# A 64-row matmul between the two passes of one block, in the second unit of both MLPs

## The chip, the cores and the metric

The kernel runs on one core of one Trainium2 chip. The metric is the device time of one execution in microseconds, as the median of several runs. Three runs of the kernel before took 2397.16, 2397.32 and 2398.94 us; the median is 2397.32 us. TensorE (PE) does the matmuls into PSUM, VectorE (DVE) and ScalarE (ACT) do the elementwise work, SyncE (SP) issues nearly all the loads.

## The reference, cut to what matters

Two layers of a decoder trunk over 256 positions of width 2048, in fp32. Each layer is a mixing part (attention and RWKV-7 in layer 0, RG-LRU and HGRN2 in layer 1) and then an MLP with squared ReLU:

```python
def _sq_relu_mlp(h, w1, w2):          # w1: 2048 x 8192, w2: 8192 x 2048
    z = jax.nn.relu(h @ w1)
    return (z * z) @ w2

x = x + _sq_relu_mlp(_rms_norm(x, norm_mlp[layer]), w_ff1[layer], w_ff2[layer])
```

The change touches only the two MLPs, and what it adds feeds none of these values.

## The kernel before, in words

Activations lie transposed: 16 tiles of 128 features by 256 positions. To keep nearly fp32 precision with single-pass matmuls, every operand is split into a rounded high part and the remainder. A moving tile is 512 columns wide: 256 of the high part, 256 of the low one.

A **unit** makes one 128-feature output tile from 16 **blocks** (`unit`, lines 155 to 161). A block handles one 128x128 piece of the weight and has two passes (`mm3`, lines 146 to 153): the **512 pass** (line 152) multiplies the high part `wh` with all 512 columns, the **256 pass** (line 153) multiplies the remainder `wl` with the 256 high columns. Both add into one PSUM bank. Each pass first loads its own 128x128 weights into the array (the PEld rows of the profile), so a block is: load `wh`, 512 pass, load `wl`, 256 pass.

The weights come in halves of a unit, 128x1024 fp32 or 512 KB. SP loads a half (line 125), ACT casts it to `wh` (line 130), DVE subtracts to get `wl` (line 132); two buffers of each exist. After the last block ACT and DVE add the two halves of the bank (lines 167, 168) and DVE applies the norm's factor and the squared ReLU.

One MLP (`mlp`) is 128 units, 64 up (`w_ff1`) and 64 down (`w_ff2`), in quarters `q` of 16 units: up(0), up(1), down(0), up(2), down(1), up(3), down(2), down(3). That is 2048 blocks per MLP. The norm before an MLP ends in one fp32 matmul with a matrix of ones (`rstd_of`, line 206, tile `ms_m`); PE runs an fp32 matmul as two rows of the trace. The scheduler places it inside the first unit, since the unit itself does not need the norm's factor.

Elsewhere fp32 matmuls of other shapes are put between the blocks of units too. In layer 0, line 425 (tile `pair`) multiplies 64-row operands with 128 columns; for each of eight head pairs it issues four such matmuls on the lower and four on the upper 64 rows. Line 350 (`lora`) uses 96 rows. The instruction order on each engine is fixed when the program is built.

Of the kernel before, what the change touches and what calls it, by code (L numbers as in the profile page):

```python
# [19 lines left out]
P = 128  # L20
T = 256
D = 2048
KT = D // P
# [35 lines left out]
def kernel(  # L59
# [20 lines left out]
    V, A, M, G = nc.vector, nc.scalar, nc.tensor, nc.gpsimd  # L80
# [19 lines left out]
    def c_(name):  # L100
        a, b = CON[name]
        return con[:, a:b]

    ident, bones, ones = c_("ident"), c_("bones"), c_("ones")
# [7 lines left out]
    def bank(name, tag="ga"):  # L112
        return pg.tile([P, 512], F32, tag=tag, name=name)
# [4 lines left out]
    def operand(pool, name):  # L118

        return [t[:, k] for t in (half_of(pool, f"{name}_{h}") for h in range(2)) for k in range(8)]  # L120
# [14 lines left out]
    def stream(src, name, pool=None):  # L135

        out = []
        for h in range(2):
            with tc.high_priority():
                out.append(split(load(src, h, name, pool if h else None), h, name))  # L140
        return out
# [5 lines left out]
    def mm3(ps, wh, wl, mv, first, last, folded=False):  # L147
        if folded:
            M.matmul(ps[:, :T], wh, mv[:, :T], start=first, stop=False)  # L149
            M.matmul(ps[:, :T], wh, mv[:, T:], start=False, stop=False)  # L150
        else:
            M.matmul(ps, wh, mv, start=first, stop=False)  # L152
        M.matmul(ps[:, :T], wl, mv[:, :T], start=False, stop=last)  # L153

    def unit(src, mv, name, folded=False, tag=None, parts=None, pool=None):
        ps = bank(f"mm_{name}", tag) if tag else pmm.tile([P, 512], F32, tag="mm", name=f"mm_{name}")
        parts = parts or stream(src, name, pool)
        for k in range(KT):
            wh, wl = parts[k // 8]
            mm3(ps, wh[:, k % 8], wl[:, k % 8], mv[k], k == 0, k == KT - 1, folded)  # L160
        return ps

    def evac(ps, name):
        t = ev.tile([P, T], F32, tag="t", name=f"t_{name}")
        s = ev.tile([P, T], F32, tag="s", name=f"s_{name}")
        with tc.high_priority():
            A.copy(t, ps[:, T:])  # L167
            V.tensor_add(s, ps[:, :T], t)  # L168
        return s
# [11 lines left out]
    def split_to(dst, src):  # L181
        A.copy(dst[:, :T], src)
        V.tensor_sub(dst[:, T:], src, dst[:, :T])
# [38 lines left out]
    def norm(name):  # L222
        acc = ev.tile([P, T], F32, tag="acc", name=f"acc_{name}", bufs=1)
        hx = operand(big, f"hx_{name}")
        return acc, hx
# [6 lines left out]
    def layer0_mix():  # L232
        with ExitStack() as st:
# [14 lines left out]
            with tc.tile_pool(name="pa", bufs=1) as pa:  # L248
# [3 lines left out]
                with tc.high_priority(10**6):  # L252
# [19 lines left out]
                    for i in range(2):  # L272
                        for j in range(8):
                            prepare(hx, 8 * i + j, xi[i][:, j], "gmix0")
                            if j == 3:
                                parts.append(split(raws[i], i, "i0_0"))
                    first.append(unit(None, hx, "i0_0", parts=parts))
                    squares(0)
                    parts = [split(raws[2], 0, "i0_1")]
                    squares(1)  # L280
                    parts.append(split(raws[3], 1, "i0_1"))
                    first.append(unit(None, hx, "i0_1", parts=parts))
                    squares(2)
                    squares(3)
                    rstd = rstd_of(acc, "a0")
                first.append(unit(w_in0[2], hx, "i0_2", tag="ga"))
                first.append(unit(w_in0[3], hx, "i0_3", tag="gb"))
                rwkv_a(pa, gate, hx, scaled_by(rstd), rwp_d, pm_d, nb, first, load_cw)
# [645 lines left out]
    def mlp(layer, xs, hx, rstd, nxt, zp, zraw):  # L934
        z = {}

        def up(q):
            zq = z[q] = operand(big if q % 2 == 0 else zp, f"z_{layer}_{q}")
            for k in range(KT):
                n = f"f1_{layer}_{q}_{k}"  # L940
                s = evac(unit(w_ff1[layer, q * KT + k], hx, n, pool=zraw), n)
                V.tensor_mul(s, s, rstd)  # L942
                V.scalar_tensor_tensor(s, s, 0.0, s, ALU.max, ALU.mult)
                split_to(zq[k], s)

        def down(q):
            for c in range(KT):
                n = f"f2_{layer}_{q}_{c}"
                s = evac(unit(w_ff2[layer, q, c], z[q], n, pool=zraw), n)
                V.tensor_add(xs[:, c], xs[:, c], s)  # L950
                if q == 3:
                    nxt(c)

        up(0)
        up(1)
        down(0)
        up(2)
        down(1)
        up(3)
        down(2)  # L960
        down(3)
# [7 lines left out]
    acc, hx = norm("m0")  # L969
# [11 lines left out]
    acc, hx = nacc  # L981
# [3 lines left out]
    acc, hx = norm("m1")  # L985
# [148 lines left out]
```

## Time and profile before

| what | us |
|---|---|
| median of three runs | 2397.32 |
| profiled execution, its own time | 2415.31 |
| its span, first to last instruction | 2413.5 |
| PE busy, share of the span | 99% |
| mean granted TensorE clock | 0.997 |

The profiled execution is one execution with the profiler on; it is 18.0 us longer than the median, and its time is 1.8 us longer than its span. In the rows, a start is counted in us from the first instruction. A matmul's own duration reaches past the start of the next one, because matmuls are pipelined; the distance between starts is what the engine needs. A line such as `x8` merges eight instructions that stand in a row.

### The profile page before, as it was taken

Reading aid. Unit: us, or ns where it says so; the run is one execution under the profiler, and the core shown is the slowest. Engines: PE = TensorE matmul, PEld = TensorE weight load, DVE = VectorE, ACT = ScalarE, POOL = GpSimd, SP = SyncE. Lnnn points to the kernel's source line nnn. Section 1 sums busy time; section 2 is a strip of 40 time slices with the busy share of each in tenths; the row PEclk is TensorE's granted clock in tenths of the full one; section 3 lists DMA queues with packets and bytes.
Section 4 is the critical chain, followed back from the end, with each engine's and each line's share of the span. In section 5 each row is a group of like instructions: output and inputs, shape, how many; then the busy total and the mean of one; then the engine's idle time right before and its main releaser. Section 6 shows DMA issues by size and latency. Waiting matters only on the chain.

```text
span 2413.5 us, 37947 instructions
## 1 busy us (share of the span) xinstructions
PE 2390.6 (99%) x14386; PEld 2072.1 (86%) x14386; DVE 1697.7 (70%) x3006; ACT 1243.7 (52%) x2152; POOL 44.9 (2%) x118
## 2 busy tenths in 40 slices
PE   8999999999999999999999999999999999999999
PEld 6888877798888888888888888889888888888888
DVE  7887865677676576576568888788777667667555
ACT  7554455555444444444456666675544444444443
POOL 0112010000000000000000000000000000000000
PEclk9999999999999999999999999999999999999999
DMA  7667743465555555655555444456556555656564
GB/s 263 212 216 228 246 139 105 155 209 183 190 184 186 188 184 187 188 185 187 187 176 187 150 151 153 154 168 217 185 191 191 189 188 191 192 187 190 191 199 134
DMA packets 125862, 446.77 MB, mean 185 GB/s; under 512 B 14192, under 2 KB 19952, under 8 KB 124016
## 3 DMA queue, kind: packets, MB, share of 16 engines
q1 hardware_dynamic: 115824, 414.06, 53.7%
q0 software_dynamic: 5456, 26.79, 3.1%
q10 hardware_dynamic: 4400, 3.50, 0.4%
q8 instruction: 114, 1.87, 0.3%
q14 instruction: 68, 0.56, 0.1%
HBM read 429.06 MB, written 15.22 MB: 184 GB/s over the span
## 4 chain that ended last, share of the span: by engine, by line
PE 93%; DVE 3%; DMA 2%; ACT 1%; issue 1%; POOL 0%; DVEq 0%; ACTq 0%; POOLq 0%
PE mm_f L152 39%; PE mm_f L153 20%; PE mm_i L152 13%; PE mm_i L153 7%; PE mm_o L153 2%; PE mm_o L152 1%; PE mm_o L149 1%; PE mm_o L150 1%; DVE wl_i L132 1%; PE hl L816 1%; PE pair L425 1%; DMA rwp<-rwp_d 1%; PE psx L496 0%; ACT wh_o L130 0%; PE psu L503 0%
## 5 line engine op out<-in xcount | busy, mean ns | idle before, releaser
L132 DVE TENSOR_TENSOR wl_f<-raw_f,wh_f 128x1024 fp32r<-128x1024 f32 x512 | 627.2, 1225 | 486.1 <-ACT wh_f L130 486.1
L130 ACT CAST wh_f<-raw_f 128x1024 fp32r<-128x1024 f32 x512 | 538.6, 1052 | 773.4 <-PE mm_f L152 566.8
L152 PE MATMUL mm_f<-hx_m,wh_f 128*128 128x512 f32 x2048 | 717.2, 395 | 0.0
L152 PE MATMUL mm_f<-z,wh_f 128*128 128x512 f32 x2048 | 717.1, 395 | 0.0
L152 PE MATMUL mm_i<-hx_a,wh_i 128*128 128x512 f32 x1536 | 563.9, 405 | 11.5 <-ACT wh_i L130 11.4
L153 PE MATMUL mm_f<-hx_m,wl_f 128*128 128x256 f32 x2048 | 574.8, 281 | 0.0
L153 PE MATMUL mm_f<-z,wl_f 128*128 128x256 f32 x2048 | 574.4, 280 | 0.0
L152 PEld LDWEIGHTS mm_f<-z,wh_f 128*128 128x128 f32 x2048 | 383.9, 187 | 90.0
L152 PEld LDWEIGHTS mm_f<-hx_m,wh_f 128*128 128x128 f32 x2048 | 383.9, 187 | 90.0
L153 PE MATMUL mm_i<-hx_a,wl_i 128*128 128x256 f32 x1536 | 447.6, 291 | 1.2 <-DVE wl_i L132 1.0
L153 PEld LDWEIGHTS mm_f<-hx_m,wl_f 128*128 128x128 f32 x2048 | 387.0, 189 | 0.1
L153 PEld LDWEIGHTS mm_f<-z,wl_f 128*128 128x128 f32 x2048 | 387.0, 189 | 0.0
L152 PEld LDWEIGHTS mm_i<-hx_a,wh_i 128*128 128x128 f32 x1536 | 289.8, 189 | 72.3 <-ACT wh_i L130 12.1
L153 PEld LDWEIGHTS mm_i<-hx_a,wl_i 128*128 128x128 f32 x1536 | 291.5, 190 | 9.3 <-DVE wl_i L132 4.0
L130 ACT CAST wh_i<-raw_i 128x1024 fp32r<-128x1024 f32 x192 | 201.3, 1049 | 188.9 <-PE mm_i L152 169.5
L132 DVE TENSOR_TENSOR wl_i<-raw_i,wh_i 128x1024 fp32r<-128x1024 f32 x192 | 234.5, 1222 | 80.6 <-ACT wh_i L130 76.4
L168 DVE TENSOR_TENSOR s_f<-mm_f,t_f 128x256 f32<-128x256 f32 x256 | 106.7, 417 | 3.0 <-ACT t_f L167 3.0
L132 DVE TENSOR_TENSOR wl_o<-raw_o,wh_o 128x1024 fp32r<-128x1024 f32 x64 | 78.3, 1223 | 32.6 <-ACT wh_o L130 32.3
L130 ACT CAST wh_o<-raw_o 128x1024 fp32r<-128x1024 f32 x64 | 67.2, 1050 | 63.3 <-issue 29.2
L167 ACT COPY t_f<-mm_f 128x256 f32<-128x256 f32 x256 | 93.2, 364 | 4.3 <-PE mm_f L153 4.3
L153 PE MATMUL mm_o<-ym,wl_o 128*128 128x256 f32 x256 | 72.6, 284 | 0.8 <-DVE wl_o L132 0.8
L942 DVE TENSOR_TENSOR s_f<-s_f,rstd_m 128x256 f32<-128x256 f32 x128 | 54.4, 425 | 4.4
(420 smaller groups left out, 2254.7 us busy)
## 6 DMA issues: line engine op xcount, KB each, us to landing
raw_f<-in_w_ff_dram SPq DMA_DIRECT2D x512, 512.0 KB, 4.5
raw_i<-in_w_in_dram SPq DMA_DIRECT2D x192, 512.0 KB, 4.1
raw_o<-in_w_out_dram SPq DMA_DIRECT2D x64, 512.0 KB, 4.2
rwp_d<-rwp POOLq DMA_DIRECT2D x8, 1026.0 KB, 7.1
rwp<-rwp_d POOLq DMA_DIRECT2D x4, 1540.0 KB, 10.7
cw<-in_cmp_w_dram SPq DMA_DIRECT2D x2, 2048.0 KB, 10.2
pm_d<-pm POOLq DMA_DIRECT2D x8, 512.0 KB, 6.3
pm<-pm_d POOLq DMA_DIRECT2D x4, 1024.0 KB, 5.3
```

What stands on the lines that cost most here:

```text
L130: A.copy(wh, raw)
L132: V.tensor_sub(wl, raw, wh)
L149: M.matmul(ps[:, :T], wh, mv[:, :T], start=first, stop=False)
L150: M.matmul(ps[:, :T], wh, mv[:, T:], start=False, stop=False)
L152: M.matmul(ps, wh, mv, start=first, stop=False)
L153: M.matmul(ps[:, :T], wl, mv[:, :T], start=False, stop=last)
L167: A.copy(t, ps[:, T:])
L168: V.tensor_add(s, ps[:, :T], t)
L425: M.matmul(pps[q][:, c * P : (c + 1) * P], bk[hs, c], ar[hs, c], start=True, stop=True)
L816: M.matmul(pl[:, x * T + i * P : x * T + (i + 1) * P], qk[:, ii], qk[:, ii], start=True, stop=True)
L942: V.tensor_mul(s, s, rstd)
```

## The change: what it does

In `mlp`, the unit with `q == 0` and `k == 1`, the second unit of each MLP, gets `part_at=4`. Its fifth block then issues its 512 pass, a new matmul of the identity's upper 64 rows with themselves (64 rows, 128 columns, fp32) into a PSUM bank of its own, and then its 256 pass. Nothing reads that bank.

```diff
+    def narrow(name):
+
+        ps = bank(f"nar_{name}")
+        tc.keep_in_program_order(M.matmul(ps[:, 0:P], ident[0:64], ident[0:64], start=True, stop=True))
+
-    def unit(src, mv, name, folded=False, tag=None, parts=None, pool=None):
+    def unit(src, mv, name, folded=False, tag=None, parts=None, pool=None, part_at=None):
...
         for k in range(KT):
             wh, wl = parts[k // 8]
+            if k == part_at:
+                M.matmul(ps, wh[:, k % 8], mv[k], start=False, stop=False)
+                narrow(name)
+                tc.keep_in_program_order(M.matmul(ps[:, :T], wl[:, k % 8], mv[k][:, :T], start=False, stop=False))
+                continue
             mm3(ps, wh[:, k % 8], wl[:, k % 8], mv[k], k == 0, k == KT - 1, folded)
...
-                s = evac(unit(w_ff1[layer, q * KT + k], hx, n, pool=zraw), n)
+                s = evac(unit(w_ff1[layer, q * KT + k], hx, n, pool=zraw, part_at=4 if q == 0 and k == 1 else None), n)
```

PE in the second unit of layer 0's MLP before, from the 256 pass of its fourth block on (`mm_f` is the unit's bank, `hx_m` the normed input, `wh_f` and `wl_f` the weights):

```order
L153 MATMUL mm_f_0_0_1_6222<-hx_m_0_5108,wl_f_0_0_1_0_6227 128x256
L152 MATMUL mm_f_0_0_1_6222<-hx_m_0_5108,wh_f_0_0_1_0_6225 128x512
L153 MATMUL mm_f_0_0_1_6222<-hx_m_0_5108,wl_f_0_0_1_0_6227 128x256
L152 MATMUL mm_f_0_0_1_6222<-hx_m_0_5108,wh_f_0_0_1_0_6225 128x512
L153 MATMUL mm_f_0_0_1_6222<-hx_m_0_5108,wl_f_0_0_1_0_6227 128x256
```

The same place on PE after the change (`nar_f` is the new bank, `con` holds the identity):

```order
L153 MATMUL mm_f_0_0_1_6222<-hx_m_0_5108,wl_f_0_0_1_0_6227 128x256
L166 MATMUL mm_f_0_0_1_6222<-hx_m_0_5108,wh_f_0_0_1_0_6225 128x512
L158 MATMUL nar_f_0_0_1_6244<-con 128x128
L168 MATMUL mm_f_0_0_1_6222<-hx_m_0_5108,wl_f_0_0_1_0_6227 128x256
L152 MATMUL mm_f_0_0_1_6222<-hx_m_0_5108,wh_f_0_0_1_0_6225 128x512
```

One row is new; the two passes around it only have new line numbers. In layer 1 the same single row is new at the same place of its second unit. No other row of any engine moves, and no instruction gets a new wait.

## Rows read from the trace of the kernel before

**Rows 1.** The page: busy time by engine; the chain that ended last, by engine.
```profile
PE 2390.6 (99%) x14386; PEld 2072.1 (86%) x14386; DVE 1697.7 (70%) x3006; ACT 1243.7 (52%) x2152; POOL 44.9 (2%) x118
...
PE 93%; DVE 3%; DMA 2%; ACT 1%; issue 1%; POOL 0%; DVEq 0%; ACTq 0%; POOLq 0%
```

**Rows 2.** Stretches, 512 passes alone: length, busy (count), PEclk, DMA share, GB/s.
```profile
600.00:1200.00 600.00, 600.00 (x1700) 319.12 (x1699) 1.00 0.59 186
1720.00:2320.00 600.00, 600.00 (x1732) 323.71 (x1731) 1.00 0.60 190
```

**Rows 3.** Groups, 566 to 1286 us (layer 0's MLP): busy, mean ns | idle before.
```profile
L152 PE MATMUL mm_f<-z,wh_f 128*128 128x512 f32 x1024 | 361.9, 399 | 0.0
...
L130 ACT CAST wh_f<-raw_f 128x1024 fp32r<-128x1024 f32 x253 | 265.7, 1050 | 385.3 <-PE mm_f L152 275.8 <-issue 109.5
```

**Rows 4.** Groups, 1703 to 2406 us (layer 1's MLP).
```profile
L152 PE MATMUL mm_f<-z,wh_f 128*128 128x512 f32 x1016 | 352.3, 391 | 0.0
...
L130 ACT CAST wh_f<-raw_f 128x1024 fp32r<-128x1024 f32 x253 | 266.6, 1054 | 381.5 <-PE mm_f L152 291.0 <-issue 90.5
```

**Rows 5.** Timeline of PE, first unit of layer 0's MLP: start, duration, instruction.
```profile
562.25 0.70 PE L206 MATMUL ms_m<-acc_m,con 128*128 128x256 f32 x2
562.60 0.47 PE L153 MATMUL mm_f<-hx_m,wl_f 128*128 128x256 f32 x1
```

**Rows 6.** Timeline of PE, first unit of layer 1's MLP.
```profile
1701.51 0.70 PE L206 MATMUL ms_m<-acc_m,con 128*128 128x256 f32 x2
1701.86 0.47 PE L153 MATMUL mm_f<-hx_m,wl_f 128*128 128x256 f32 x1
```

**Rows 7.** Timeline of PE, layer 0's input projection, 64-row matmuls before a 256 pass.
```profile
81.84 0.39 PE L152 MATMUL mm_i<-hx_a,wh_i 128*128 128x512 f32 x1
82.16 1.16 PE L425 MATMUL pair<-rwp,bk 64*128 64x128 f32 x8
83.25 0.39 PE L153 MATMUL mm_i<-hx_a,wl_i 128*128 128x256 f32 x1
83.47 0.39 PE L152 MATMUL mm_i<-hx_a,wh_i 128*128 128x512 f32 x1
```

**Rows 8.** Timeline of PE, the first two and last two of those eight.
```profile
82.16 0.49 PE L425 MATMUL pair<-rwp,bk 64*128 64x128 f32 x2
...
82.94 0.38 PE L425 MATMUL pair<-rwp,bk 64*128 64x128 f32 x2
```

**Rows 9.** Groups, 84.5 to 95.8 us, after the return of rows 7.
```profile
L152 PE MATMUL mm_i<-hx_a,wh_i 128*128 128x512 f32 x34 | 11.8, 391 | 0.0
```

**Rows 10.** Timeline of PE, a return from 64-row matmuls to a 512 pass.
```profile
175.07 0.72 PE L425 MATMUL pair<-rwp,bk 64*128 64x128 f32 x5
175.72 0.50 PE L152 MATMUL mm_i<-hx_a,wh_i 128*128 128x512 f32 x1
```

**Rows 11.** Groups, 177 to 186 us, after the return of rows 10.
```profile
L152 PE MATMUL mm_i<-hx_a,wh_i 128*128 128x512 f32 x25 | 8.9, 398 | 0.0
```

**Rows 12.** Timeline of PE, a return from 96-row matmuls to a 256 pass.
```profile
47.46 0.60 PE L350 MATMUL lora<-th,w 96*128 96x256 f32 x2
47.97 0.39 PE L153 MATMUL mm_i<-hx_a,wl_i 128*128 128x256 f32 x1
48.19 0.40 PE L152 MATMUL mm_i<-hx_a,wh_i 128*128 128x512 f32 x1
```

**Rows 13.** Groups, 39.6 to 46.6 and 49.5 to 56 us, before and after rows 12.
```profile
L152 PE MATMUL mm_i<-hx_a,wh_i 128*128 128x512 f32 x21 | 7.5, 399 | 0.0
...
L152 PE MATMUL mm_i<-hx_a,wh_i 128*128 128x512 f32 x20 | 7.0, 391 | 0.0
```

**Rows 14.** Timeline of PE, output projection of layer 1, after a short stall.
```profile
1613.24 0.39 PE L153 MATMUL mm_o<-ym,wl_o 128*128 128x256 f32 x1
1613.46 0.39 PE L152 MATMUL mm_o<-ym,wh_o 128*128 128x512 f32 x1
```

**Rows 15.** Groups, 1614 to 1620 us, after rows 14.
```profile
L152 PE MATMUL mm_o<-ym,wh_o 128*128 128x512 f32 x18 | 6.4, 399 | 0.0
```

**Rows 16.** Stretch from layer 0's MLP to layer 1's, 512 passes alone (columns of rows 2).
```profile
1290.00:1700.00 410.00, 323.48 (x883) 166.09 (x884) 1.00 0.52 170
```

## The prediction

> **What bounds the kernel now.** I read the page first: PE is busy for 99% of the span and makes 93% of the chain that ended last [rows 1], so what matters is how fast PE takes its blocks. Then I put one stretch of each MLP beside the other. They do the same work in the same code, yet 600 us hold 1700 512 passes in layer 0 and 1732 in layer 1 [rows 2]. A block thus takes 600/1700 = 352.9 ns in layer 0 and 600/1732 = 346.4 ns in layer 1: 6.5 ns apart (the two counts can be off by one, 0.2 ns each). The granted clock is 1.00 in both, the 2.4 GHz level [rows 2]. The groups by line give a fingerprint of the two cadences: a 512 pass lasts 399 ns on average in the slow one and 391 ns in the quick one [rows 3, 4]. Neither MLP lets PE wait: idle before the passes is 0.0 [rows 3, 4]. It is ACT that waits for PE to free weight buffers, 275.8 us in layer 0 and 291.0 us in layer 1 [rows 3, 4], so weights are not what makes layer 0 slow.
>
> What differs is the last disturbance before each stretch. In both MLPs it is the norm's matmul with full 128 rows, and PE returns from it through a 256 pass 0.35 us later [rows 5, 6]. The rows look alike, and yet one MLP stays slow for its whole length and the other quick. I read the cadence as something that a disturbance sets and that an undisturbed stream then keeps.
>
> **The change, part by part.** It removes nothing and moves nothing. It adds one 64-row fp32 matmul per MLP, which is a disturbance, and the question is which cadence follows.
>
> *The cadence after it.* The nearest rows are those of line 425, also 64 rows by 128 columns in fp32, between the passes of a unit. Where PE returns from them to a 256 pass [rows 7], the next stretch runs at 391 ns [rows 9]. There are three more such returns with a long stretch behind them (at 106, 129 and 152 us), and all run at 391. Where PE returns to a 512 pass [rows 10], the stretch runs at 398 ns [rows 11]; two more of these (at 200 and 227 us) run at 399. So with 64 rows the side of return decides: 4 of 4 quick through the 256 pass, 3 of 3 slow through the 512 pass. The change returns through the 256 pass. A quick cadence in layer 0 gives 6.5 ns for each block behind the insertion, of which there are 2048 - 16 - 5 = 2027: 2027 x 6.52 ns = 13.2 us. In layer 1 the stretch is quick already and stays so: 0.
>
> All four of these returns came from a quick stream, while layer 0's MLP is slow. The nearest row from a slow stream has 96 rows instead of 64: 399 ns before it, return through a 256 pass, 391 ns behind it [rows 12, 13]. The Trainium skill bears on this: "TensorEngine Tiling (Array Packing)", Key Properties, says that a change of tiling mode drains the engine. If so, the return would start from an empty array, and the cadence before would not matter; no row shows a 64-row matmul in a slow stream.
>
> *The cost of each insertion.* Rows 7 give the parts. From the 512 pass to the first 64-row row: 82.16 - 81.84 = 0.32 us. From the 256 pass to the next 512 pass: 83.47 - 83.25 = 0.22 us. The eight rows between take 83.25 - 82.16 = 1.09 us; they are four matmuls, two rows each, and the new one has two rows. The first two end at 82.65 and the last two at 83.32, and the 256 pass starts 0.07 us before that end [rows 8, 7]; so two rows alone take 0.49 - 0.07 = 0.42 us. Sum 0.32 + 0.42 + 0.22 = 0.96 us in place of 0.35 us: 0.61 us more. The bounds are 2/8 of 1.09 us, thus 0.27 in place of 0.42 (0.46 us more), and all 1.09 us (1.28 us more). I take 0.61 us, the value of rows of the same shape. Two insertions cost 1.2 us (0.9 to 2.6). All of it lies on PE, which has no idle time to hide it.
>
> *Weights at the quicker pace.* ACT and DVE must supply layer 0 at 346.4 ns a block; in layer 1 they do so with PE idle 0.0 and with ACT waiting 291.0 us for PE [rows 4]. I cost that at nothing. If the cover were gone, it would eat a part of the 13.2 us, never more.
>
> *What follows.* Layer 1's mixing part begins 13 us earlier and its stalls will fall otherwise. Its 883 512 passes [rows 16] run partly in each cadence; if half of them changed sides, that is 883/2 x 6.5 ns = 2.9 us either way. I take 0 and keep 2.9 us for the range.
>
> *The sum.* -13.2 + 1.2 = -12.0 us against the profiled execution: 2415.3 becomes 2403.3 us. The median of the runs is 18.0 us below the profiled time. If the runs have the same cadences as the profile, the profiler itself costs 18.0 us, and the median becomes 2397.3 - 12.0 = 2385.3 us.
>
> **The rivals.**
>
> *Both MLPs slow in the runs.* Nothing but a small difference around the norm's matmul seems to separate the MLPs [rows 5, 6], so layer 1 could be slow where no profiler runs. Then both insertions gain: -26.4 + 1.2, 2372.1 us. Against it: the profiler would then cost 18.0 + 13.2 = 31.2 us.
>
> *Nothing to repair.* Both MLPs are quick already in unprofiled runs; the 18.0 us by which the median lies below the profiled time has room for the 13.2 us. Then the insertions only cost: 2397.3 + 1.2 = 2398.5 us. The same time results if the cadence belongs to the place (buffers, addresses) and no disturbance changes it; against that stands that one projection with the same tiles shows both, 399 and 391 ns [rows 13]. The same time also results if a pass had a fixed distance to the next, as it has in neither MLP [rows 2]. The Trainium skill has such a rule: "TensorE: Matmul & The Clock Gate", Back-to-back issue gap, gives columns / 2.4 + 2.5 ns, an estimate of 325 ns for a block whatever came before; both measured cadences lie above it.
>
> *The restart falls slow.* The point that decides is the first two or three blocks behind the insertion. A return through a 256 pass after a short stall, with the same 0.22 us to the next 512 pass, was followed by 399 ns [rows 14, 15], and the return after the norm's matmul of layer 0 as well [rows 5, 3]. If both insertions end so, layer 0 stays slow and layer 1 loses its quick cadence: 13.2 + 1.2 = 14.4 us more, 2411.7 us. If only layer 1's does, layer 0's gain cancels it, and 2398.5 us results again. Against it: none of the four long 64-row returns to a 256 pass did this.
>
> **How the numbers follow.** I give the forecast (2385.3) a chance of 0.50, both MLPs slow (2372.1) 0.12, nothing to repair or one cancelling the other (2398.5) 0.24, the slow restart (2411.7) 0.14. Differences under 0.2%, 4.8 us, cannot be told from no change here. Faster: 0.50 + 0.12 = 0.62; same 0.24; slower 0.14. The likeliest case's own range is 2381 to 2390 us (the 2.9 us, the insertion's bounds, the counts). The range of 8 in 10 leaves out the slow restart and reaches over the other three with a small margin: 2370 to 2401 us.
>
> **What would show it.** In the profile of the changed kernel: the new matmul stands as two rows between a 512 and a 256 pass at about 567 us, with some 0.96 us from that 512 pass to the next. The 512 passes behind it average 391 ns, and 600 us of layer 0's MLP hold 1732 of them, not 1700. Layer 0's MLP ends about 12.6 us earlier, and layer 1's stays at 391 ns. The forecast is wrong if either MLP shows 399 ns behind its insertion, if PE starts to wait for weights, or if layer 0's MLP is quick and the time of the runs does not fall, which would mean that the runs were quick before.

## The result, and the profile after

The changed kernel takes 2426.17 us (median of four runs, 2425.75 to 2426.64); the kernel before, timed beside it, takes 2397.24 us. The ratio is 1.0119, with an interval of 1.0102 to 1.0137: 28.9 us slower, where 12 us faster were forecast.

The stretches of the profile after, for the 512 passes alone (columns as in [rows 2]):

```profile
600.00:1200.00 600.00, 600.00 (x1699) 319.06 (x1698) 1.00 0.58 187
1760.00:2360.00 600.00, 600.00 (x1699) 319.07 (x1698) 1.00 0.59 187
```

Both MLPs are now slow: 1699 blocks in 600 us, where [rows 2] had 1700 in layer 0 and 1732 in layer 1. The clock is again 1.00. The counts include a pass that only reaches into the stretch, so 600 us divided by them comes out 0.2 to 0.4 ns too low. Taken from the starts of the 512 passes, a slow block takes 353.33 ns on average and a quick one 346.67 ns, 6.67 ns apart. No slow block takes 353 ns, though: three blocks of 349, 350 and 361 ns follow each other in turn, 1060 ns in all, where three quick ones take 1040 ns. The timeline of PE in layer 0's MLP shows the turn (start, duration, instruction):

```profile
562.50 0.39 PE L152 MATMUL mm_f<-hx_m,wh_f 128*128 128x512 f32 x1
562.73 0.28 PE L153 MATMUL mm_f<-hx_m,wl_f 128*128 128x256 f32 x1
562.85 0.39 PE L166 MATMUL mm_f<-hx_m,wh_f 128*128 128x512 f32 x1
563.17 0.49 PE L158 MATMUL nar_f<-con 64*128 64x128 f32 x2
563.59 0.39 PE L168 MATMUL mm_f<-hx_m,wl_f 128*128 128x256 f32 x1
563.81 0.39 PE L152 MATMUL mm_f<-hx_m,wh_f 128*128 128x512 f32 x1
564.04 0.28 PE L153 MATMUL mm_f<-hx_m,wl_f 128*128 128x256 f32 x1
564.15 0.40 PE L152 MATMUL mm_f<-hx_m,wh_f 128*128 128x512 f32 x1
564.40 0.28 PE L153 MATMUL mm_f<-hx_m,wl_f 128*128 128x256 f32 x1
```

Ahead of the new matmul the 512 passes last 0.39 us: this execution came out of the norm's matmul quick in layer 0, unlike that of [rows 3, 5]. The insertion costs what was worked out: 563.81 - 562.85 = 0.96 us for that block. The second block behind it shows the change of pace: from its 512 pass at 564.15 to its 256 pass the starts lie 241 ns apart (0.25 us by the rounded rows), where a quick stream has 230 ns, and from there to the end of the MLP the 512 passes last 399 ns on average. Groups, 564 to 1280 us and 1704 to 2420 us; these rows answer to [rows 3] and [rows 4]:

```profile
L152 PE MATMUL mm_f<-z,wh_f 128*128 128x512 f32 x1024 | 362.0, 399 | 0.0
```

Both stretches give this same row. To see where the 28.9 us lie, I compare with a second profile of the kernel before, taken in an execution of 2397.5 us (its first profile was of one that took 2415.3). The two norm matmuls mark the stages; the rows below give the first and last start of their weight loads. The kernel before:

```profile
L206 PEld LDWEIGHTS ms_m<-acc_m,con x4: 186/188/190, 557.8 to 1683.8; 128*128 128x128 f32 x4
L206 PEld LDWEIGHTS ms_a<-acc_a,con x4: 188/188/192, 25.6 to 1271.6; 128*128 128x128 f32 x4
```

The changed kernel:

```profile
L216 PEld LDWEIGHTS ms_m<-acc_m,con x4: 186/188/190, 558.4 to 1698.4; 128*128 128x128 f32 x4
L216 PEld LDWEIGHTS ms_a<-acc_a,con x4: 187/188/191, 26.1 to 1286.4; 128*128 128x128 f32 x4
```

| stage | before | after | difference |
|---|---|---|---|
| up to the norm of layer 0's MLP | 557.8 | 558.4 | 0.6 |
| layer 0's MLP | 713.8 | 728.0 | 14.2 |
| layer 1's mixing part | 412.2 | 412.0 | -0.2 |
| layer 1's MLP, to the span's end | 711.8 | 726.0 | 14.2 |

Of the 28.8 us between the two spans 28.4 lie in the two MLPs, in equal parts. Per MLP, 2027 blocks x (353.33 - 346.67) ns = 13.5 us and the insertion's 0.6 us make 14.1 us, against 14.2 in the table.

### The profile page after: what moved, and what is told of

The parts are those of the page before. It is cut to its first block, busy times and chain, and to the rows that moved or that the text cites. A ratio compares the mean times of both kernels' runs of the same rounds, so it can differ in the third digit from the quotient of the medians.

```text
span 2424.4 us, 37955 instructions
## 1 busy us (share of the span) xinstructions
PE 2401.3 (99%) x14390; PEld 2071.0 (85%) x14390; DVE 1698.4 (70%) x3006; ACT 1243.3 (51%) x2152; POOL 44.9 (2%) x118
## 4 chain that ended last, share of the span: by engine, by line
PE 93%; DVE 3%; DMA 2%; ACT 1%; issue 1%; POOL 0%; DVEq 0%; ACTq 0%; POOLq 0%
PE mm_f L152 40%; PE mm_f L153 20%; PE mm_i L152 13%; PE mm_i L153 7%; PE mm_o L153 2%; PE mm_o L152 1%; PE mm_o L149 1%; PE mm_o L150 1%; DVE wl_i L132 1%; PE hl L826 1%; PE pair L435 1%; DMA rwp<-rwp_d 1%; PE psx L506 0%; ACT wh_o L130 0%; DMA raw_o<-in_w_out_dram 0%
## 5 line engine op out<-in xcount | busy, mean ns | idle before, releaser
L953 DVE SCALAR_TENSOR_TENSOR s_f<-s_f 128x256 f32<-128x256 f32 x128 | 54.4, 425 | 4.4
```

## The experiments

### The kernel before, profiled again

No edit.

> The kernel before, once more, with a second profile. Theory 1 (both MLPs run in the quick cadence in most executions; the first profile was an execution with a slow layer 0): both MLPs show 512 passes of 391 ns, 1732 in 600 us, and the profiled time lies near 2397 us. Theory 2 (the profile's cadences are also those of the runs, and the profiler costs 18 us): again 399 ns in layer 0, 391 ns in layer 1 and a profiled time near 2415 us, with the runs at 2397.

Measured: 2397.14 us (2395.61 to 2409.89); the profiled execution took 2397.46 us. Its stretches:

```profile
600.00:1200.00 600.00, 600.00 (x1732) 323.94 (x1731) 1.00 0.56 190
1760.00:2360.00 600.00, 600.00 (x1732) 323.91 (x1731) 1.00 0.57 192
```

Both MLPs are quick, and the profiler costs next to nothing. Theory 1 holds. The norm's rows in the first profile and one stretch of it (512 passes alone) show where its 18.0 us were:

```profile
L206 PEld LDWEIGHTS ms_m<-acc_m,con x4: 186/188/189, 562.2 to 1701.6; 128*128 128x128 f32 x4
L206 PEld LDWEIGHTS ms_a<-acc_a,con x4: 188/188/188, 25.9 to 1289.7; 128*128 128x128 f32 x4
300.00:340.00 40.00, 17.35 (x46) 8.83 (x45) 0.87 0.35 113
```

Layer 0's MLP took 1289.7 - 562.2 = 727.5 us there and 713.8 in the second profile: 13.7 us, the slow cadence. Another 4.4 us (562.2 against 557.8) lie ahead of it, where the granted clock averaged 0.87 from 300 to 340 us and 1.00 in the second profile.

The times of the kernel before spread as theory 1 demands. Of its 77 executions timed beside the kernels of this document, 20 took more than 2407 us. Of these, 17 lie from 2407.8 to 2412.4, some 13 us above the others, 16 of them at a granted clock of 1.00. That fits one slow MLP; it is inferred from the times, since of the executions in that band no trace was kept.

### The new matmul in layer 0 alone

```diff
-part_at=4 if q == 0 and k == 1 else None
+part_at=4 if layer == 0 and q == 0 and k == 1 else None
```

> The new matmul in layer 0's MLP alone. Theory 1 (each insertion turns its own MLP from quick to slow, 2027 blocks x 6.5 ns + 0.6 us = 13.8 us): about 2411 us, 399 ns in layer 0 and 391 ns in layer 1. Rival (the loss of 29 us has one source, in layer 0 or in layer 1 alone, or comes from something that the second MLP inherits): near 2397 or near 2426 us.

Measured: 2410.21 us, 13.2 us above 2396.98 for the kernel before beside it (ratio 1.0051, 1.0030 to 1.0072). One of its executions took 6778.93 us, which nothing here explains; the ratio leaves it out. The stretches:

```profile
600.00:1200.00 600.00, 600.00 (x1699) 319.21 (x1698) 1.00 0.55 186
1760.00:2360.00 600.00, 600.00 (x1732) 323.80 (x1731) 1.00 0.57 191
```

Each insertion makes its own MLP slow, and the second MLP inherits nothing.

### The same matmul before a 512 pass

```diff
             if k == part_at:
-                M.matmul(ps, wh[:, k % 8], mv[k], start=False, stop=False)
                 narrow(name)
+                tc.keep_in_program_order(M.matmul(ps, wh[:, k % 8], mv[k], start=False, stop=False))
...
```

> The same 64-row matmul, one pass later or earlier in the sequence: behind a 256 pass and ahead of the next 512 pass, in both MLPs. Theory 1 (the side of the return decides, as the rows of before had it, where returns to a 512 pass were slow 3 of 3): slow in both, about 2426 us. Theory 2 (what decides is the exact moment of the return within a few ns, so the side alone says nothing): quick in one or both is possible, 2398 or 2412 us. Theory 3 (any 64-row matmul inside an MLP ends slow, because of the place): 2426 us.

Measured: 2424.97 us (ratio 1.0114, 1.0084 to 1.0143), slow in both MLPs (1699 and 1700 blocks in 600 us). By itself this fits theories 1 and 3 and does not contradict 2. In the changed kernel the return to a 256 pass was slow as well, so the side alone does not decide.

### Two, three and four matmuls

```diff
-        tc.keep_in_program_order(M.matmul(ps[:, 0:P], ident[0:64], ident[0:64], start=True, stop=True))
+        for i in range(4):
+            tc.keep_in_program_order(M.matmul(ps[:, i * P : (i + 1) * P], ident[0:64], ident[0:64], start=True, stop=True))
```

> Four 64-row matmuls, eight rows, in place of one, at the same place before the 256 pass: the count that line 425 has in the mixing part, where 4 of 4 long returns were quick. Theory 2 (the moment of the return decides, and eight rows bring it as line 425 does): quick in both MLPs, about 2397 + 2 x (0.6 + 6 x 0.11) = 2399.8 us, 391 ns. Theory 3 (the place, inside an MLP, decides): slow in both, about 2427.5 us, 399 ns.

Measured: 2399.0 us (ratio 0.9998, 0.9976 to 1.0021). The ratio is not that of the two medians: the long executions of the kernel before count in it too. The timeline and the stretches, with eight rows in place of two:

```profile
561.39 0.39 PE L167 MATMUL mm_f<-hx_m,wh_f 128*128 128x512 f32 x1
561.71 1.16 PE L159 MATMUL nar_f<-con 64*128 64x128 f32 x8
562.79 0.39 PE L169 MATMUL mm_f<-hx_m,wl_f 128*128 128x256 f32 x1
563.01 0.39 PE L152 MATMUL mm_f<-hx_m,wh_f 128*128 128x512 f32 x1
```

```profile
600.00:1200.00 600.00, 600.00 (x1732) 323.83 (x1731) 1.00 0.56 190
1760.00:2360.00 600.00, 600.00 (x1732) 323.82 (x1732) 1.00 0.57 192
```

Four matmuls at the same place keep both MLPs quick, as the eight rows of [rows 7] did. So it is not the place, and theory 3 falls. For two and three matmuls the loop runs over `range(2)` and `range(3)`.

> Two 64-row matmuls, four rows, in place of one, before the 256 pass in both MLPs. Four matmuls left both MLPs quick (2399.0 us), one left both slow (2426.2 us). Theory A (one matmul is the exception: its two rows are both edge rows, and any steady row between sets the return right): quick in both, 2397 + 2 x 0.83 = 2398.7 us. Theory B (the return hits a moment that each added row shifts by a fraction of a ns, and four matmuls happened to hit it): slow in one or both, 2412 to 2427 us.

Measured: 2397.84 us (ratio 0.9993, 0.9974 to 1.0012), 1732 blocks in both stretches.

> Three 64-row matmuls, six rows. Theory A (all counts above one are quick): 2397 + 2 x 1.05 = 2399.1 us, 391 ns in both MLPs. Theory B (it alternates or scatters with the count): slow, 2426 to 2428 us.

Measured: 2425.26 us (ratio 1.0116, 1.0088 to 1.0143), 1699 blocks in both. One and three are slow, two and four quick. Theory A (any count above one) falls; B's scatter is a strict alternation so far.

### 128 rows in place of 64

```diff
-ident[0:64], ident[0:64]
+ident, ident
```

> One matmul of the whole identity, 128 rows, in place of the 64-row one, at the same place. Theory C (the slow cadence comes from the change of rows, which empties the engine at both ends): the short way in and out without it leaves the cadence quick, 2397 + 2 x 0.25 = 2397.7 us. Theory B (any disturbance may end on either side, by the moment of its return): slow is as possible, 2412 or 2425 us.

Measured: 2426.64 us (ratio 1.0125, 1.0089 to 1.0162), 1700 blocks in both stretches. Theory C falls: a matmul that uses all rows makes both MLPs slow too. The slow cadence needs no change of rows.

### From a slow stream

```diff
-                narrow(name)
+                narrow(name, 1 if name.endswith("_1") else 4)
...
-part_at=4 if q == 0 and k == 1 else None
+part_at=4 if q == 0 and k in (1, 3) else None
```

> One 64-row matmul in the second unit of each MLP, as in the changed kernel, and four of them in the fourth unit, so that the second disturbance meets a slow stream. Theory 2 (the return alone sets the cadence, whatever came before): slow for the 32 blocks between, quick behind them, 2397 + 2 x (0.6 + 1.3 + 0.2) = 2401.2 us. Rival (the cadence before it is handed on, and four matmuls only kept a quick one): slow in both, about 2428 us.

Measured: 2399.95 us (ratio 1.0006, 0.9990 to 1.0022). Groups in layer 0's MLP, between the two disturbances (562.5 to 572.5 us) and behind the second (576 to 1200 us):

```profile
L152 PE MATMUL mm_f<-hx_m,wh_f 128*128 128x512 f32 x30 | 10.6, 399 | 0.0
```

```profile
L152 PE MATMUL mm_f<-hx_m,wh_f 128*128 128x512 f32 x967 | 335.4, 391 | 0.0
```

The single matmul sets the slow cadence, the four undo it. A slow stream can be repaired: that part of the prediction's idea was right.

### 126, 124 and 120 columns

The odd and even counts asked for a reason. Every added matmul moves the return by two rows of 111.7 ns. The two cadences differ by 6.67 ns, and the quick one is 52 times that; I call 6.67 ns a **tick**. When the starts of the 512 passes of one execution are taken modulo a tick, all quick stretches of nine or more passes in even steps lie at one position, with a slow drift (in the trace after: twelve stretches from 27 to 559 us at 0.50 to 0.35 of a tick, nine from 1394 to 1699 us at 0.15 to 0.10). Of ninety steps from 346.67/20 to 346.67/109 ns only the tick and its half bring the stretches together like this, in each of four traces. A few quick stretches step by 343 and 350 ns in turn and so lie at two positions, half a tick apart. And 223.3 ns is 33.5 ticks. So I changed the moment of the return without changing the number of matmuls:

```diff
-ps[:, 0:P], ident[0:64], ident[0:64]
+ps[:, 0:126], ident[0:64], ident[0:64, 0:126]
```

> One 64-row matmul as in the changed kernel, with 126 columns in place of 128, so that the return comes some ns earlier and nothing else differs. Theory G (all quick streams of one execution start on one grid of 346.7/52 = 6.67 ns; the cadence hangs on where between two ticks the return falls; one and three matmuls, slow, and two and four, quick, differ by 2 x 111.7 = 223.3 ns = 33.5 ticks, thus by half a tick): if both rows get 0.83 ns shorter per column, 2 columns are 3.3 ns, half a tick, and both MLPs turn quick, 2397 + 1.2 = 2398 us; if only the last row does, a quarter of a tick, side open. Rival N (the number of matmuls as such, odd or even, decides): slow in both, 2426 us.

Measured: 2400.49 us (ratio 0.9976, 0.9947 to 1.0006), 1732 blocks in both stretches.

> The same with 124 columns. Theory G: if both rows get shorter, 4 columns are 6.7 ns, a whole tick, and both MLPs stay slow, 2426 us; if only the last row does, half a tick, and both turn quick, 2398 us. Of 126 and 124 columns, one at least turns quick. Rival N (odd or even number): slow, 2426 us.

Measured: 2398.58 us (ratio 0.9984, 0.9958 to 1.0010), 1732 blocks in both.

> The same with 120 columns: the control for whole ticks. Theory G: two whole ticks or one (13.3 or 6.7 ns), so both MLPs are slow again, 2426 us, whichever way 126 and 124 went. Rival (a shorter matmul as such is quick): 2398 us.

Measured: 2426.61 us (ratio 1.0095, 1.0068 to 1.0121), 1699 blocks in both. The stretches of 124 columns:

```profile
600.00:1200.00 600.00, 600.00 (x1732) 323.70 (x1731) 1.00 0.59 190
1760.00:2360.00 600.00, 600.00 (x1732) 323.62 (x1732) 1.00 0.60 192
```

and of 120:

```profile
600.00:1200.00 600.00, 600.00 (x1699) 319.05 (x1698) 1.00 0.59 187
1760.00:2360.00 600.00, 600.00 (x1699) 319.09 (x1699) 1.00 0.59 187
```

Four columns less turn 28 us of loss into none, and eight bring it back. Rival N falls, and theory G holds with only one of the two rows getting shorter. The two slow column counts are multiples of 8 and the two quick ones are not; a rule of that kind is not excluded by these three runs, but it would leave two and four matmuls of 128 columns unexplained. The distance from the last 512 pass ahead of the insertion to the 256 pass behind it, from the starts in the traces, puts the 64-row insertions into a quick stream on one line:

| insertion | ns | ticks of 6.67 ns | both MLPs |
|---|---|---|---|
| 120 columns | 728, 729 | 109.2, 109.4 | slow |
| 124 columns | 731, 732 | 109.7, 109.8 | quick |
| 126 columns | 733 | 110.0 | quick |
| 128 columns (the change) | 735 | 110.3 | slow |
| two matmuls | 958 | 143.7 | quick |
| three matmuls | 1181 | 177.2 | slow |
| four matmuls | 1405 | 210.8 | quick |

Starts are read to 1 ns, 0.15 of a tick. A fraction of 0.2 to 0.4 ended slow, 0.7 to 1.0 quick.

The distance serves only where the last 512 pass itself starts on a tick, that is in a steady quick stream. The second profile of the kernel before holds a return of the kind of [rows 7] that shows this (timeline, then the group from 153 to 162 us):

```profile
150.55 1.16 PE L425 MATMUL pair<-rwp,bk 64*128 64x128 f32 x8
```

```profile
L152 PE MATMUL mm_i<-hx_a,wh_i 128*128 128x512 f32 x26 | 9.2, 399 | 0.0
```

It comes 1412 ns, 211.8 ticks, after its 512 pass and yet is slow. Only three 512 passes stand ahead of it, 356 and 343 ns apart. Measured from the ticks on which the quick streams around it start, it falls at 0.50. Read in this way, line 425's returns to a 256 pass with a long stretch behind them, four in each of 14 traces, fit theory G: 52 of 56 fall at 0.69 to 0.80 and are quick, the other 4 fall at 0.46 to 0.55 and are slow. The insertions of the table fall at 0.20 to 0.30 (slow) and 0.70 to 0.96 (quick). The four matmuls behind a slow stream, whose distance of 1414 ns is 212.1 ticks, fall at 0.78 to 0.80 and are quick. The 128-row matmul falls at 0.40 and is slow. This reading came after the runs; what was on record before them is that 120 columns are slow and that one at least of 126 and 124 is quick.

### Two matmuls before a 512 pass

The edit of the 512 side and that of two matmuls together.

> Two 64-row matmuls between a 256 pass and the next 512 pass. One matmul there was slow (2425.0 us). Theory G with the moment alone: the return falls half a tick later, so it may well turn quick, 2397 + 2 x 0.85 = 2398.7 us. Rival (the side of the return counts as well: the rows of before had eight rows before a 512 pass slow 3 of 3, and four rows fall on the same half tick as eight): slow in both, 2426.5 us.

Measured: 2426.64 us (ratio 1.0097, 1.0070 to 1.0121), 1700 and 1699 blocks. The half tick that rescued the other side does not rescue this one: the side counts as well. The rule of [rows 10, 11] held in 7 of 7 returns: 3 in the first trace, and one in each MLP of the two kernels here. Line 425 returns to a 512 pass 42 times in all 14 traces, and all 42 are slow.

## Why the prediction was wrong

*The cadence in the profile is that of the runs* (the sum's last step): wrong. The first profile caught an execution with a slow layer 0, 13.7 us of the 18.0. In most executions both MLPs are quick, so there was nothing to gain. The prediction had this as the rival "nothing to repair", but gave it 0.24 and took the 18.0 us for the profiler's cost. The second profile, at 2397.46 us, shows that the profiler costs nothing of that size.

*A return to a 256 pass is quick* (the step on the cadence): wrong, and this decided the sign. "4 of 4" was four copies of one case: all had eight rows, so all returned 1405 ns after the last 512 pass. In the second profile of the same kernel it was 3 of 4. The 96-row return of [rows 12, 13] was a single case as well: it was quick in 9 of the 14 traces and slow in 5. The new matmul has two rows and returns at 735 ns, half a tick elsewhere. I used the eight rows only to price the insertion and did not ask whether the moment of return could matter; the counterexamples of [rows 14, 15] and [rows 5], which are returns to a 256 pass that ended slow, said that the side is not enough.

*A return to a 512 pass is slow*: right, on both half ticks tried.

*A disturbance sets the cadence and a stream keeps it*: right (the repair from a slow stream, and each MLP by itself). The Trainium skill states that a change of tiling mode drains the engine ("TensorEngine Tiling (Array Packing)", Key Properties). The traces fit this: from the 512 pass to the inserted matmul it is 320 ns with 64 rows and 230 with 128, and from its last row to the 256 pass 201 and 31 ns. But such a drain does not make the return neutral: a 64-row matmul leaves either cadence, and a 128-row one gives the slow one too.

*The price of the slow cadence*: 13.2 us per MLP forecast, 13.6 measured (14.2 less the insertion). *The price of an insertion*: 0.61 us forecast, 0.61 measured. *Weights at the quicker pace, and layer 1's mixing part*: nothing and within 2.9 us forecast; PE idle stayed 0.0 and the mixing part moved by 0.2 us.

*The rivals*: the restart that falls slow was what happened, but priced from a layer 0 that was slow already, 2411.7 us. "Nothing to repair" and "falls slow" are independent, and their joint case was missing: 2397.3 + 2 x (13.2 + 0.6) = 2424.9 us, against 2426.2 measured.

## What to carry to other kernels

When two equal stretches of one profile run at different paces, profile a second execution before pricing a repair: the pace may change between executions. Samples that repeat one geometry count as one sample. If a stream of weight loads and matmuls must keep its quick pace, put a disturbance of fixed length just ahead of it and tune its length by a few columns: the variants that returned right (two or four matmuls, 124 or 126 columns, four after a slow stream) took at most 2406.3 us in 50 of 50 executions, where the kernel before went above 2407 us in 20 of 77. Their medians do not beat the kernel before's beyond their intervals; what they remove, by these times, is the occasional slow MLP.

## What the runs showed of the hardware that I had not expected

The same stream of blocks has two stable paces at one granted clock of 1.00: 346.7 and 353.3 ns on average, one 6.67 ns tick apart. After a 64-row matmul that returns to a 256 pass, which one it takes hangs on the moment of the return within that tick, and then it lasts for some 2000 blocks. What runs in steps of 6.67 ns, and why the return to a 512 pass was slow at both half ticks, the runs do not show.

Other disturbances have other limits. Of the 28 returns from the norm's matmul in the 14 traces, 27 fall at 0.30 to 0.99 of a tick and are quick; the one of the first profile's layer 0 falls at 0.16 and is slow. That matmul has to wait for DVE's `acc_m` and starts 397 to 425 ns after the 512 pass ahead of it, while the inserted one always starts 320 ns behind a quick stream. So its moment differs between executions. That this is where the slow executions of the kernel before come from is likely, but rests on that one slow return. For the 128-row matmul and plain stalls no limits were tried.
